# The last two projections of an encoder trunk, as seven block products on pairs of token tiles

## Chip, core, metric

The kernel runs on one core of a Trainium2 chip. The metric is the device time of one execution in microseconds, the median of the runs. The core's engines are TensorE (PE in the profile: matmuls; PEld: its weight loads), VectorE (DVE), ScalarE (ACT), GpSimd (POOL) and SyncE (SP), which here only issues transfers. Each engine works through its own instructions in order.

## What is computed

The reference is a two-layer encoder trunk on 2048 + 256 tokens of 1024 channels, in f32. Cut to the part that is touched, the end of layer 1 (mixer C, its output projection, the residual, and the gate of the per-layer embedding):

```
y = (mixed * c_scale) * silu(g)                  # mixer C
h = h + y @ w_out                                # output projection, 1024 x 1024
gate = sigmoid(rms_norm(h, norm_ple[1]) @ w_ple_gate[1])       # the last gate, 1024 x 1024
out = h + gate * (p[1] @ w_ple_proj[1])          # the last product is made early, and kept in DRAM
```

Layer 0 ends with the same gate on its own weights, and its result is the `h` that mixer C reads.

## The kernel before

Tokens are worked on in 18 tiles of 128 (`P`). Every f32 matrix product is made of three matmuls: each operand is held as a rounded high part and the remainder, a low part, and `mm3` (L177 to L179) adds high times high, high times low and low times high in PSUM. A split is a cast on ScalarE and a subtraction on VectorE (`split_ps` for results in PSUM, L117 and L118; `split_w` for weights, L127 and L128, with a gain L130 and L131) or both on GpSimd (`split_po`, L121 and L122).

Three stages stand at the end of the program, and the order of their work is that in which a scheduler has put the code's instructions on each engine:

- The first gate's loop (layer 0, from about 2366 to 2610 us): a token tile takes 48 matmuls of 512 columns (`gate_half`, L945 on, twice 24 into `po` and `pf`) and eight transposes of the next tile's normed rows. `norm_rows` is a Square with a sum on ScalarE (L184), and on GpSimd a small scale (L109), a power (L112) and the scaling of the tile (L186).
- Mixer C (to about 3035 us): nine blocks of 256 tokens, four channel groups each. Its result goes to DRAM as high and low halves (`ycT_d`).
- The final stage, `out_ple` (L1021 to L1066): for each token tile, `head` makes the output projection in 48 matmuls (two halves of the columns into `pa`), VectorE adds it to the residual `xr` (L1048), the sum is normed and transposed, and `gate_half` makes 48 matmuls of the gate (L957 the sigmoid, L958 and L959 the product with `pp` and the sum). The loop works on the projection of the next tile and the gate of this one by turns.

So the final stage has 18 x 96 = 1728 matmuls of 128x512. The matmul's tiles stand in the trace as `pa<-wh,yh`: PSUM tile, then the streamed weights and the stationary activations. In this stage the weights lie in pools opened on the left side of the memory; `yh` and `yl` come from `work`, a pool on the right; `nh` and `nl` come from the pool `opw1`, on the left. In the first gate's loop weights and activations both lie on the right.

## Time and profile before

| what | value |
|---|---|
| three runs | 3454.49, 3457.00, 3457.43 us, median 3457.0 us |
| the profiled execution | 3456.42 us, of which the span of instructions is 3454.6 us |
| TensorE | busy 3389.5 us, 98% of the span, mean granted clock 0.996 |
| VectorE, ScalarE, GpSimd | busy 57%, 49%, 49% |

The times of single instructions below all come from the one profiled execution, so a sum of them is to be held against its 3456.42 us: the span plus 1.8 us around it. Shares of busy time are averages over very different stages, and what bounds a stage is read in that stage.

### The profile page before, as it was taken

Reading aid. Unit: us, or ns where it says so; the run is one execution under the profiler, and the core shown is the slowest. Engines: PE = TensorE matmul, PEld = TensorE weight load, DVE = VectorE, ACT = ScalarE, POOL = GpSimd, SP = SyncE. Lnnn points to the kernel's source line nnn. Section 1 sums busy time; section 2 is a strip of 40 time slices with the busy share of each in tenths; the row PEclk is TensorE's granted clock in tenths of the full one; section 3 lists DMA queues with packets and bytes.
Section 4 is the critical chain, followed back from the end, with each engine's and each line's share of the span. In section 5 each row is a group of like instructions: output and inputs, shape, how many; then the busy total and the mean of one; then the engine's idle time right before and its main releaser. Section 6 shows DMA issues by size and latency. Waiting matters only on the chain.

```text
span 3454.6 us, 60128 instructions
## 1 busy us (share of the span) xinstructions
PE 3389.5 (98%) x21694; PEld 3020.9 (87%) x21694; DVE 1974.1 (57%) x4298; ACT 1675.6 (49%) x3100; POOL 1694.9 (49%) x1997
## 2 busy tenths in 40 slices
PE   9999999999999999999999999998999999999999
PEld 8998999998899988888888887886889999988887
DVE  5346666667767677768779788773434222342222
ACT  4325666666666666546767776552324111221111
POOL 6774545454645455446777777761113445420000
PEclk9999999999999999999999999999999999999999
DMA  9654323234423324664445635337534122353332
GB/s 289 200 165 137 109 79 105 85 104 126 143 81 100 90 77 123 173 190 124 134 133 158 177 97 140 126 95 258 177 130 158 61 74 68 103 166 111 116 110 73
DMA packets 473969, 446.12 MB, mean 129 GB/s; under 512 B 34504, under 2 KB 414920, under 8 KB 472648
## 3 DMA queue, kind: packets, MB, share of 16 engines
q1 hardware_dynamic: 473672, 442.28, 41.7%
q8 instruction: 172, 2.82, 0.3%
q14 instruction: 125, 1.02, 0.1%
HBM read 277.53 MB, written 164.63 MB: 128 GB/s over the span
## 4 chain that ended last, share of the span: by engine, by line
PE 88%; DVE 4%; DMA 3%; issue 2%; ACT 1%; POOL 1%; SPq 0%; DVEq 0%; ACTq 0%; POOLq 0%
PE pf L177 10%; PE pf L178 10%; PE pf L179 10%; PE pt L369 9%; PE pa L407 6%; PE pa L408 6%; PE po L177 6%; PE po L178 6%; PE po L179 6%; PE pa L177 4%; PE pa L178 4%; PE pa L179 4%; PE po L501 3%; PE po L500 3%; DVE s L653 1%
## 5 line engine op out<-in xcount | busy, mean ns | idle before, releaser
L419 ACT ACTIVATE s<-s,mx 128x1024 f32<-128x1024 f32 x512 | 585.7, 1147 | 172.9 <-DVE mx L653 88.0
L377 DVE TENSOR_TENSOR pl<-pt,ph 128x512 fp32r<-128x512 f32 x780 | 524.1, 686 | 202.3 <-ACT ph L373 194.1
L373 ACT CAST ph<-pt 128x512 fp32r<-128x512 f32 x780 | 437.0, 584 | 261.6 <-PE pt L369 126.5
L369 PE MATMUL pt<-ident,s 128*128 128x128 f32 x3120 | 467.3, 273 | 5.7 <-DVE pl L377 4.5
L369 PEld LDWEIGHTS pt<-ident,s 128*128 128x128 f32 x3120 | 369.5, 140 | 56.6 <-issue 7.0
L653 DVE CUSTOM_DVE_ANT_0 s<-pa,dist,mx 128x512 f32<-128x512 f32 x384 | 286.2, 746 | 51.1 <-PE pa L408 36.1
L673 POOL TENSOR_TENSOR s<-s 128x1024 f32<-128x1024 f32 (+1 forms) x136 | 315.2, 2335 | 0.2
L109 POOL TENSOR_SCALAR rstd<-ss 128x1 f32<-128x1 f32 (+1 forms) x64 | 15.5, 242 | 605.4 <-ACT xn L184 583.6
L482 POOL TENSOR_SCALAR s<-s,rs 128x1024 f32<-128x1024 f32 (+1 forms) x272 | 298.0, 1107 | 12.1
L472 DVE TENSOR_SCALAR_CACHE_REDUCE s<-pa,mx 128x512 f32<-128x512 f32 x384 | 286.1, 745 | 23.1 <-PE pa L408 13.9
L500 PE MATMUL po<-ph,vA 128*128 128x256 f32 x1040 | 282.2, 293 | 0.6 <-ACT ph L373 0.6
L501 PE MATMUL po<-pl,vA 128*128 128x256 f32 x1040 | 279.5, 295 | 1.1 <-DVE pl L377 1.1
L177 PE MATMUL pf<-xh,wh 128*128 128x256 f32 x944 | 265.5, 281 | 2.5 <-DMA xh<-xTh_d 2.5
L178 PE MATMUL pf<-xl,wh 128*128 128x256 f32 x944 | 266.2, 282 | 0.2 <-DMA xl<-xTl_d 0.2
L179 PE MATMUL pf<-xh,wl 128*128 128x256 f32 x944 | 265.3, 281 | 0.0
L407 PE MATMUL pa<-kk,q 128*128 128x512 f32 (+1 forms) x528 | 220.1, 419 | 14.5 <-DMA q<-qTl_d 6.0
L407 PE MATMUL pa<-kA,q 128*128 128x512 f32 (+1 forms) x528 | 222.3, 421 | 3.5 <-DVE s L472 3.3
L112 POOL TENSOR_TENSOR rstd<-rstd,mhalf 128x1 f32<-128x1 f32 (+3 forms) x154 | 164.6, 1069 | 110.5 <-DVE rstd L111 93.3
L958 DVE TENSOR_TENSOR sg<-pp,sg 128x512 f32<-128x512 f32 x72 | 49.8, 692 | 289.8 <-ACT sg L957 284.9
L408 PE MATMUL pa<-kA,q 128*128 128x512 f32 (+1 forms) x528 | 208.1, 394 | 0.0
L408 PE MATMUL pa<-kk,q 128*128 128x512 f32 (+1 forms) x528 | 207.3, 395 | 0.1
L500 PEld LDWEIGHTS po<-ph,vA 128*128 128x128 f32 x1040 | 196.9, 189 | 10.4 <-ACT ph L373 1.0
(240 smaller groups left out, 9753.2 us busy)
## 6 DMA issues: line engine op xcount, KB each, us to landing
xr<-h_d SPq DMA_DIRECT2D x54, 512.0 KB, 3.3
q<-qTh_d SPq DMA_DIRECT2D x144, 128.0 KB, 3.0
q<-qTl_d SPq DMA_DIRECT2D x144, 128.0 KB, 3.0
xh<-xTh_d SPq DMA_DIRECT2D x18, 1024.0 KB, 5.4
xl<-xTl_d SPq DMA_DIRECT2D x18, 1024.0 KB, 8.2
h_d<-xr SPq DMA_DIRECT2D x72, 256.0 KB, 3.6
pp_d<-xr SPq DMA_DIRECT2D x72, 256.0 KB, 2.3
pp<-pp_d SPq DMA_DIRECT2D x36, 512.0 KB, 3.8
```

Source lines behind the costliest of these rows:

```text
L177: pe.matmul(out, lhsT=lhs[0], rhs=rhs[0], start=first, stop=False)
L178: pe.matmul(out, lhsT=lhs[0], rhs=rhs[1], start=False, stop=False)
L179: pe.matmul(out, lhsT=lhs[1], rhs=rhs[0], start=False, stop=last)
L369: pe.transpose(pt[:, (c * 2 + i) * P : (c * 2 + i + 1) * P], s[:, (c0 + c) * P : (c0 + c + 1) * P], ident)
L373: ac.copy(ph, pt)
L377: ve.tensor_tensor(out=pl, in0=pt, in1=ph.bitcast(F32), op=ALU.subtract)
L407: pe.matmul(ps, lhsT=q1, rhs=k[:, i * 512 : i * 512 + w], start=True, stop=False)
L408: pe.matmul(ps, lhsT=q2, rhs=k[:, i * 512 : i * 512 + w], start=False, stop=True)
L419: ac.activation(s[:, c], s[:, c], AF.Exp, bias=bias, scale=-1.0, accum_out=sums[i])
L500: pe.matmul(ov[0][:, 0:256], lhsT=v, rhs=ph[:, c], start=c0 + c == 0, stop=False)
L501: pe.matmul(ov[0][:, 0:256], lhsT=v, rhs=pl[:, c], start=False, stop=c0 + c == nk - 1)
L653: ve.tensor_tensor_reduce(out=s[:, c : c + w], in0=ps, in1=dist[:, off + c : off + c + w], op0=ALU.add, op1=ALU.min, scale=slope, scalar=3 ...
```

## The change

The fused final stage is replaced by two passes over nine pairs of token tiles: first the output projection of all pairs (`n` = 0), whose sum `h` is written back to `h_d`, then the gate of all pairs (`n` = 1), which loads it again. In each pass a pair's 256x1024 times 1024x1024 product is cut into 2x2 blocks, where the two rows of blocks are the pair's two tiles, and made by Strassen's scheme (Winograd's form) with seven products of 128 tokens, 512 channels and 512 columns instead of eight. A product is 4 chunks of 3 matmuls, so a pair takes 84 matmuls of 128x512, and both passes 18 x 84 = 1512.

For that, sums and differences of blocks are needed on both sides. Those of the weights (`t0` to `t3`, four for each matrix) are made on GpSimd in `halves_sums`, called in eight steps of the first gate's loop, written to DRAM, and loaded and split like weights by `block_w`. The 28 split chunks of the gate's blocks go into the tiles of the output projection's, each as soon as its last use, in the last pair of the first pass, is over. The sums of the activations (`s1` to `s4`) are made in `Pair.prepare`: in the first pass on GpSimd, with the low parts on VectorE, in the second on VectorE from the transposed rows in PSUM, with the low parts on GpSimd. `Pair.use` adds the products up, mostly on VectorE, and `Pair.end` makes sigmoid (ScalarE), product with `pp` (GpSimd) and the last sum (VectorE). Mixer C stores its result as one f32 tensor (no `split_po`), and `xn` has two buffers.

The diff, cut to its core:

```diff
-    ycT_d = [dscratch(f"ycT{i}_d", [D, T]) for i in "hl"]
+    ycT_d = dscratch("ycT_d", [D, T])
+    t_d = [[dscratch(f"t{n}{i}_d", [512, 512]) for i in range(4)] for n in "og"]
...
+    def part(src, low):
+        hi, lo = (work.tile([P, 512], F32R, tag=f"a{x}", name=f"a{x}", bufs=8) for x in "hl")
+        ac.copy(hi, src)
+        low.tensor_tensor(out=lo, in0=src, in1=hi.bitcast(F32), op=ALU.subtract)
+        return hi.rearrange("p (c t) -> p c t", t=P), lo.rearrange("p (c t) -> p c t", t=P)
...
+        return [part(quarter(xn, k), ve) for k in range(2)]
...
+    w_tail = ins["w_out_c"][0], ins["w_ple_gate"][1]
+    def halves_sums(pool, n, c):
+        q = []
+        for i in range(4):
+            k, a = divmod(i, 2)
+            b = pool.tile([P, 512], F32, tag=f"q{i}", name="q", bufs=2)
+            sy.dma_start(b, w_tail[n][k * 512 + c * P : k * 512 + c * P + P, a * 512 : a * 512 + 512])
+            if n:
+                ac.activation(b, b, AF.Copy, scale=gple[1][:, k * 4 + c : k * 4 + c + 1])
+            q.append(b)
+        b11, b12, b21, b22 = q
+        for i, (out, x, y) in enumerate(((b11, b12, b11), (b12, b22, b12), (b22, b22, b11), (b21, b21, b22))):
+            po.tensor_tensor(out=out, in0=x, in1=y, op=ALU.subtract)
+            sy.dma_start(t_d[n][(0, 2, 1, 3)[i]][c * P : c * P + P], out)
...
+    BLK = ["11", "21", "t1", "t0", "22", "t3", "t2"]
+    HOME = dict(zip(BLK, ((0, 0), (1, 0), (1, 4), (2, 0), (2, 4), (3, 0), (3, 4))))
...
+    def block_w(n, b):
+        got = []
+        for c in range(4):
+            hi, lo = pair_w(HOME[b][0], HOME[b][1] + c)
+            st = slot()
+            if b[0] == "t":
+                sy.dma_start(st, t_d[n][int(b[1])][c * P : c * P + P])
+                ac.copy(hi, st)
+                (po if c % 2 else ve).tensor_tensor(out=lo, in0=st, in1=hi.bitcast(F32), op=ALU.subtract)
+            else:
+                k, a = int(b[0]) - 1, int(b[1]) - 1
+                sy.dma_start(st, w_tail[n][k * 512 + c * P : k * 512 + c * P + P, a * 512 : a * 512 + 512])
+                split_w(st, hi, lo, gple[1][:, k * 4 + c : k * 4 + c + 1] if n else None)
+            got.append((hi, lo))
+        return got
...
+        def prepare(self):
+            t0, n = self.t0, self.n
+            self.xr, xn = [], []
+            for tq in (t0, t0 + P):
+                self.xr.append(loaded(tq))
+                if not n:
+                    y = work.tile([P, D], F32, tag="xn", name="yc")
+                    sy.dma_start(y.rearrange("p (c t) -> p c t", t=P), chans(ycT_d, tq, P))
+                    xn.append(y)
+            if n:
+                xn = [norm_rows(work, x) for x in self.xr]
+            yield
+            def at(i, k):
+                return quarter(xn[i], k) if n else xn[i][:, k * 512 : k * 512 + 512]
+            e, low = (ve, po) if n else (po, ve)
+            a21 = at(1, 0)
+            if n:
+                t = temp()
+                ac.copy(t, a21)
+                a21 = t
+            yield
+            a11 = at(0, 0)
+            self.a11 = part(a11, ve)
+            s3 = temp()
+            e.tensor_tensor(out=s3, in0=a11, in1=a21, op=ALU.subtract)
+            yield
+            a22 = at(1, 1)
+            s2 = temp()
+            e.tensor_tensor(out=s2, in0=a22, in1=s3, op=ALU.subtract)
+            e.tensor_tensor(out=a21, in0=a22, in1=a21, op=ALU.add)
+            self.s2 = part(s2, low)
+            self.s1 = part(a21, low)
+            self.a22 = part(a22, ve)
+            yield
+            a12 = at(0, 1)
+            self.a12 = part(a12, ve)
+            e.tensor_tensor(out=s2, in0=a12, in1=s2, op=ALU.subtract)
+            self.s3 = part(s3, low)
+            yield
+            self.s4 = part(s2, low)
+            yield
...
+        def end(self, g, i, a):
+            cols, x, t = slice(a * 512, a * 512 + 512), self.xr[i], self.t0 + i * P
+            ac.activation(g, g, AF.Sigmoid)
+            (ve if self.last and a == 0 else po).tensor_tensor(out=g, in0=self.pp[i][:, cols], in1=g, op=ALU.mult)
+            def late():
+                ve.tensor_tensor(out=x[:, cols], in0=x[:, cols], in1=g, op=ALU.add)
+                sy.dma_start(rows(yout, t, P)[:, cols], x[:, cols])
+            after.append(late)
...
+            if m == 1:
+                self.u = gsum()
+                ac.copy(self.u, ps)
+                if not n:
+                    plus(x[0][0], x[0][0])
+            elif m == 2:
+                if n:
+                    g = gsum()
+                    plus(g, self.u)
+                    self.end(g, 0, 0)
                 else:
-                    WG += load_w(wp[g], ins["w_ple_gate"][layer][k : k + 512], 512, [(0, D)], "wg",
-                                 gple[layer][:, k // P : k // P + 4])
-
-            def head(tq):
-                yh = work.tile([P, KC, P], F32R, tag="yh", name="yh")
-                yl = work.tile([P, KC, P], F32R, tag="yl", name="yl")
-                load2(yT, (yh[:, :kc], yl[:, :kc]), lambda d: d[k0:D, tq : tq + P].rearrange("(c p) t -> p c t", p=P))
-                xr = work.tile([P, D], F32, tag="xr", name="xr", bufs=NXR)
-                sy.dma_start(xr, h_d[tq : tq + P])
-                for a in (0, 512):
-                    ps = pa()
-                    for c in range(kc):
-                        mm3(ps, (yh[:, c], yl[:, c]), (WO[c][0][:, a : a + 512], WO[c][1][:, a : a + 512]), c == 0, c == kc - 1)
-                    ve.tensor_tensor(out=xr[:, a : a + 512], in0=ps, in1=xr[:, a : a + 512], op=ALU.add)
-                    if a == 0:
-                        yield
-                yield xr, norm_rows(work, xr, 1)
-
-            nxt = list(head(0))[1]
-            for tq in range(0, T, P):
-                xr, xn = nxt
-                nh = pw.tile([P, KC, P], F32R, tag="nh", name="nh", bufs=1)
-                nl = pw.tile([P, KC, P], F32R, tag="nl", name="nl", bufs=1)
-                step = head(tq + P) if tq + P < T else iter((None, None))
-                next(step)
-                transpose_rows(xn, nh, nl, 0)
-                nxt = next(step)
-                sg = [pw.tile([P, D], F32, tag="sg", name="sg", bufs=1)]
-                for a, pg in ((0, po_()), (512, pf_())):
-                    gate_half(pw, layer, WG, (nh, nl), tq, a, pg, sg, xr, dst(tq))
-
-
-    with pool_ as ws:
-        wp += [ws.enter_context(tc.tile_pool(name=f"wc{g}", bufs=1, reuse_waits="tile")) for g in range(1, 4)]
-        pc = ws.enter_context(tc.tile_pool(name="plc", bufs=1, reuse_waits="tile"))
+                    plus(x[0][0], x[0][0])
+            elif m == 6:
+                plus(self.u, self.u)
+                if not n:
+                    plus(x[1][0], x[1][0], self.u, po)
+            elif m == 5:
+                self.v = gsum()
+                plus(self.v, self.u)
+                if not n:
+                    plus(x[0][1], x[0][1], self.v, po)
+                    plus(x[1][1], x[1][1], self.v, po)
+            elif m == 3:
+                if n:
+                    g = gsum()
+                    plus(g, self.v)
+                    self.end(g, 0, 1)
+                else:
+                    plus(x[0][1], x[0][1])
+                    sy.dma_start(h_d[self.t0 : self.t0 + P], self.xr[0])
+            elif m == 4:
+                to = self.u if n else x[1][0]
+                plus(to, to)
+                if self.last:
+                    self.end(to, 1, 0)
+            elif n:
+                plus(self.u, self.u)
+                if not self.last:
+                    self.end(self.u, 1, 0)
+                plus(self.v, self.v)
+                self.end(self.v, 1, 1)
+            else:
+                plus(x[1][0], x[1][0])
+                plus(x[1][1], x[1][1])
+                sy.dma_start(h_d[self.t0 + P : self.t0 + 2 * P], self.xr[1])
...
+    pairs = [Pair(n, t0) for n in range(2) for t0 in range(0, T, 2 * P)]
...
+    ahead_c = (lambda: None, lambda: begin(BLK[:1], 0), lambda: begin(BLK[1:3], 4), lambda: begin(BLK[3:5], 2))
...
-                split_po(mx[:, :, :cnt], yh[:, :, :cnt], yl[:, :, :cnt])
-                store2(ycT_d, (yh[:, :, :cnt], yl[:, :, :cnt]),
-                       lambda d: d[g * 256 : g * 256 + 256, t0 - 8 + oa : t0 - 8 + ob].rearrange("(m p) t -> p m t", p=P))
+                sy.dma_start(ycT_d[g * 256 : g * 256 + 256, t0 - 8 + oa : t0 - 8 + ob].rearrange("(m p) t -> p m t", p=P), mx[:, :, :cnt])
...
+    begin(BLK[5:], 0)
+    for i, p in enumerate(pairs):
+        step = pairs[i + 1].prepare() if i + 1 < len(pairs) else iter(())
+        order = list(zip((1, 2, 6, 5, 3, 4, 7), BLK))
+        for m, b in order[:5] + order[:4:-1] if p.last else order:
+            a = getattr(p, {1: "a11", 2: "a12", 6: "s2", 5: "s1", 3: "s4", 4: "a22", 7: "s3"}[m])
+            ps = {2: po_, 4: po_, 5: pf_, 7: pf_}.get(m, pa)()
+            for c in range(4):
+                mm3(ps, (a[0][:, c], a[1][:, c]), W[p.n][b][c], c == 0, c == 3)
+            flush_()
+            if m == 1 and p.n:
+                p.embedding()
+            p.use(m, ps)
+            if m != 2:
+                next(step, None)
+            if p.n == 0 and pairs[i + 1].n:
+                W[1][b] = block_w(1, b)
+    flush_()
```

On TensorE, the final stage of before: the end of a gate half, the projection's first half with the transposes behind it, and the start of the gate (`yh`, `yl`, `nh`, `nl` as above).

```order
L179 MATMUL pf<-wh,nl 128x512
L177 MATMUL pa<-wh,yh 128x512 [waits DMAHW0_49]
L178 MATMUL pa<-wl,yh 128x512
L179 MATMUL pa<-wh,yl 128x512 [waits DMAHW1_49]
...
L199 MATMUL pt<-ident,xn 128x128 [waits Pool_49]
L199 MATMUL pt<-ident,xn 128x128 x3
L199 MATMUL pt<-ident,xn 128x128 [waits PE_49]
L199 MATMUL pt<-ident,xn 128x128 x3
L177 MATMUL pa<-wh,yh 128x512
...
L177 MATMUL po<-wh,nh 128x512 [waits Activation_49]
L178 MATMUL po<-wl,nh 128x512
L179 MATMUL po<-wh,nl 128x512 [waits DVE_49]
```

The same engine in the change, a pair of the second pass, from the end of its fifth product (`pa`) over the sixth (`po`) and the seventh (`pf`) to the first of the next pair (`ah` and `al` are the parts of a block or a sum of blocks of activations).

```order
L180 MATMUL pa<-wh,al 128x512
L984 MATMUL pt<-ident,xn 128x128 [waits PE_49]
L984 MATMUL pt<-ident,xn 128x128 x3
L178 MATMUL po<-wh,ah 128x512 [waits DVE_49]
L179 MATMUL po<-wl,ah 128x512
L180 MATMUL po<-wh,al 128x512
...
L984 MATMUL pt<-ident,xn 128x128 [waits Activation_49]
L984 MATMUL pt<-ident,xn 128x128 x3
L178 MATMUL pf<-wh,ah 128x512 [waits DVE_49]
...
L178 MATMUL pa<-wh,ah 128x512 [waits Activation_49]
L179 MATMUL pa<-wl,ah 128x512
L180 MATMUL pa<-wh,al 128x512 [waits DVE_49]
```

The next pair's transposes stand in three groups near the end of a pair (the first group, of eight, is a few rows above this piece), no longer in one per tile, and all matmuls take their activations from `work`.

On GpSimd, two steps of the first gate's loop before: nothing but the norm (in the final stage its rows are the same).

```order
L109 TENSOR_SCALAR rstd<-ss 128x1 [waits Activation_49]
L112 TENSOR_TENSOR rstd<-rstd,mhalf 128x1 [waits Pool_49]
L186 TENSOR_SCALAR xn<-xr,rstd 128x1024 [waits DMAHW0_49,PE_49,Pool_49]
L109 TENSOR_SCALAR rstd<-ss 128x1 [waits Activation_49]
L112 TENSOR_TENSOR rstd<-rstd,mhalf 128x1 [waits Pool_49]
L186 TENSOR_SCALAR xn<-xr,rstd 128x1024 [waits DMAHW1_49,PE_49,Pool_49]
```

The same loop in the change, where the block sums of the weights (`q`) begin.

```order
L187 TENSOR_SCALAR xn<-xr,rstd 128x1024 [waits DMAHW1_49,PE_49,Pool_49]
L1041 TENSOR_TENSOR q<-q 128x512 [waits DMAHW4_49,DMAHW5_49,DMAHW3_49,DMAHW6_49,DMAHW2_49,DMAHW7_49,DMAHW1_49,DVE_49]
L1041 TENSOR_TENSOR q<-q 128x512 [waits DMAHW4_49,DMAHW7_49,DVE_49,Pool_49]
L1041 TENSOR_TENSOR q<-q 128x512 [waits DMAHW0_49,PE_49,Pool_49]
...
L1041 TENSOR_TENSOR q<-q 128x512 [waits DMAHW4_49,DMAHW1_49,DMAHW0_49]
L1041 TENSOR_TENSOR q<-q 128x512 [waits DMAHW6_49,DMAHW4_49,Pool_49]
L1041 TENSOR_TENSOR q<-q 128x512 [waits Pool_49]
L110 TENSOR_SCALAR rstd<-ss 128x1 [waits Activation_49]
L113 TENSOR_TENSOR rstd<-rstd,mhalf 128x1 [waits Pool_49]
L187 TENSOR_SCALAR xn<-xr,rstd 128x1024 [waits DMAHW6_49,PE_49,Pool_49]
```

Eleven of the 32 subtractions now stand in one piece between two norms; five of those between the dots are left out.

On GpSimd again, the change where the second pass begins (`wl<-st,wh` is the low part of a chunk of weights, `al<-tmp,ah` that of a sum of activations, `xr<-g,xr` a sum of the first pass).

```order
L1183 TENSOR_TENSOR xr<-g,xr 128x512
L1100 TENSOR_TENSOR wl<-st,wh 128x512 [waits DMAHW1_49,PE_49,Activation_49]
L1100 TENSOR_TENSOR wl<-st,wh 128x512 [waits DMAHW3_49,PE_49,Activation_49]
L110 TENSOR_SCALAR rstd<-ss 128x1 [waits Activation_49]
L977 TENSOR_TENSOR al<-tmp,ah 128x512 [waits Activation_49]
L113 TENSOR_TENSOR rstd<-rstd,mhalf 128x1 [waits Pool_49]
L977 TENSOR_TENSOR al<-tmp,ah 128x512 [waits Activation_49]
L1100 TENSOR_TENSOR wl<-st,wh 128x512 [waits DMAHW5_49,PE_49,Activation_49]
L187 TENSOR_SCALAR xn<-xr,rstd 128x1024 [waits PE_49,Pool_49]
L977 TENSOR_TENSOR al<-tmp,ah 128x512 [waits Activation_49]
L977 TENSOR_TENSOR al<-tmp,ah 128x512 [waits PE_49,Activation_49]
```

Low parts of weights, of activations and the norm's three steps now share this queue, where before the norm alone stood.

## Rows read from the trace of the kernel before

**Rows 1.** The page: busy times, then the chain that ended last.
```profile
PE 3389.5 (98%) x21694; PEld 3020.9 (87%) x21694; DVE 1974.1 (57%) x4298; ACT 1675.6 (49%) x3100; POOL 1694.9 (49%) x1997
...
PE 88%; DVE 4%; DMA 3%; issue 2%; ACT 1%; POOL 1%; SPq 0%; DVEq 0%; ACTq 0%; POOLq 0%
```

**Rows 2.** Windows: start:end, length; busy us of PE, PEld, DVE, ACT, POOL; clock.
```profile
2366.50:2645.00 278.50, 268.11 (x1358) 226.33 (x1357) 119.12 (x204) 100.88 (x200) 49.44 (x75) 0.99 0.53 176
2645.00:3035.00 390.00, 390.00 (x3348) 390.00 (x3348) 110.85 (x240) 80.53 (x142) 188.80 (x242) 1.00 0.25 81
3035.00:3454.60 419.60, 414.30 (x1877) 339.53 (x1875) 108.23 (x163) 68.96 (x119) 43.79 (x62) 1.00 0.37 112
```

**Rows 3.** TensorE's waits from 3035 us on: us in total, times, longest.
```profile
PE po L177 <- ACT nh L117: 0.3, 1, 0.3
```

**Rows 4.** Timeline of TensorE: start us, length us, instruction; rows of one tile.
```profile
3199.16 0.39 PE L177 MATMUL po<-wh,nh 128*128 128x512 f32 x1
...
3201.88 0.39 PE L177 MATMUL pf<-wh,nh 128*128 128x512 f32 x1
...
3207.32 0.39 PE L177 MATMUL pa<-wh,yh 128*128 128x512 f32 x1
...
3212.92 1.03 PE L199 MATMUL pt<-ident,xn 128*128 128x128 f32 x8
...
3214.03 0.39 PE L178 MATMUL pa<-wl,yh 128*128 128x512 f32 x1
...
3230.30 0.39 PE L177 MATMUL pa<-wh,yh 128*128 128x512 f32 x1
```

**Rows 5.** Timeline of TensorE: first and last matmul of the final stage.
```profile
3035.32 0.40 PE L177 MATMUL pa<-wh,yh 128*128 128x512 f32 x1
...
3449.20 0.39 PE L179 MATMUL pf<-wh,nl 128*128 128x512 f32 x1
```

**Rows 6.** Groups by line from 3035 us on: busy us, mean ns of one.
```profile
L1048 DVE TENSOR_TENSOR xr<-pa,xr 128x512 f32<-128x512 f32 x36 | 24.9, 691 | 122.2 <-PE pa L179 122.2
L186 POOL TENSOR_SCALAR xn<-xr,rstd 128x1024 f32<-128x1024 f32 x18 | 20.3, 1127 | 1.9
L117 ACT CAST nh<-pt 128x512 fp32r<-128x512 f32 x36 | 19.3, 590 | 90.1 <-PE pt L199 90.1
L184 ACT ACTIVATE xn<-xr 128x1024 f32<-128x1024 f32 x18 | 19.1, 1061 | 95.8 <-issue 79.5 <-DVE xr L1048 16.4
L112 POOL TENSOR_TENSOR rstd<-rstd,mhalf 128x1 f32<-128x1 f32 x18 | 9.9, 549 | 1.5
```

**Rows 7.** Splits by source line: ns at least, median, at most; first and last.
```profile
L122 POOL TENSOR_TENSOR yl<-mixd,yh x36: 1239/1290/1764, 2640.4 to 3050.3; 128x512 fp32r<-128x512 f32 x28, 128x496 fp32r<-128x496 f32 x4, 128x528 fp32r<-128x528 f32 x4
L127 ACT CAST wh<-st x16: 610/622/626, 3002.5 to 3021.5; 128x512 fp32r<-128x512 f32 x16
L128 DVE TENSOR_TENSOR wl<-st,wh x16: 670/690/1527, 3003.1 to 3022.8; 128x512 fp32r<-128x512 f32 x16
L130 ACT ACTIVATE wh<-st,gple x32: 709/723/732, 2323.3 to 3047.1; 128x512 fp32r<-128x512 f32 x32
L131 DVE SCALAR_TENSOR_TENSOR wl<-st,gple,wh x32: 737/751/1571, 2324.7 to 3049.0; 128x512 fp32r<-128x512 f32 x32
```

**Rows 8.** Timelines of VectorE, then GpSimd, over the same stretch.
```profile
3037.62 5.25 DVE L131 SCALAR_TENSOR_TENSOR wl<-st,gple,wh 128x512 fp32r<-128x512 f32 x4 [1.78 <-ACT wh L130]
...
3039.44 4.59 POOL L1132 TENSOR_TENSOR zz<-zz 128x536 f32<-128x536 f32 x3
```

**Rows 9.** TensorE's waits in the first gate's loop, 2360 to 2640 us.
```profile
PE po L177 <- ACT sg L957: 4.2, 1, 4.2
PE pt L199 <- POOL xn L186: 1.8, 2, 1.0
```

**Rows 10.** Timelines of ScalarE and VectorE: the last instructions.
```profile
3449.63 0.60 ACT L957 ACTIVATE sg<-pf 128x512 f32<-128x512 f32 x1 [1.67 <-PE pf L179]
...
3450.26 0.69 DVE L958 TENSOR_TENSOR sg<-pp,sg 128x512 f32<-128x512 f32 x1 [0.78 <-ACT sg L957]
```

More of the change, by code (lines that the diff above doesn't have):

```diff
@@ L1011, in trunk_kernel @@
         else:
-            x0 = [work.tile([P, KC, NB], F32R, tag=t, name="x0") for t in ("yh", "yl")]
-            transpose_rows(xn, *x0, 0)
-            xn = norm_rows(work, loaded(P), 1)
+            first_x.append(norm_rows(work, loaded(P)))
         gate_half(pw, 0, WG0, n_, tq, 512, pf_(), sg, xr[0], h_d[tq : tq + P])
@@ new lines, in trunk_kernel, with begin @@
+    pairs = [Pair(n, t0) for n in range(2) for t0 in range(0, T, 2 * P)]
+    W = [{}, {}]
+    first_step = pairs[0].prepare()
+    def begin(blocks, steps):
+        for b in blocks:
+            W[0][b] = block_w(0, b)
+        for _ in range(steps):
+            next(first_step)
+    ahead_c = (lambda: None, lambda: begin(BLK[:1], 0), lambda: begin(BLK[1:3], 4), lambda: begin(BLK[3:5], 2))
+    for g in range(1, 4):
+        load_c(g)
+    with tc.tile_pool(name="plc", bufs=1, reuse_waits="tile") as pc:
@@ L1070, in trunk_kernel @@
         edge = pc.tile([P, 4, 16], F32, name="edge")
         sy.dma_start(edge, ins["pool_edge"].rearrange("w e -> (w e)").partition_broadcast(P).rearrange("p (w e) -> p w e", e=16))
-        for g in range(1, 4):
-            load_c(wp[g], g)
         zc = pc.tile([P, 4, 2, 16], F32, name="zc")
@@ L1077, in chain @@
         def chain(t0):
-            xh = work.tile([P, KC, NB], F32R, tag="yh", name="xh")
-            xl = work.tile([P, KC, NB], F32R, tag="yl", name="xl")
-            for tt in range(NB // P):
-                transpose_rows(norm_rows(work, loaded(t0 + tt * P), 1), xh, xl, tt * P)
-            return xh, xl
+            return turned2([norm_rows(work, loaded(t0 + tt * P)) for tt in range(2)])
         ZW = NB + 24
```

114 lines of the change are left out of this document (77 added, 37 removed).

## Prediction, made before the changed kernel was run

> **What bounds the kernel now.** I read the page first: TensorE is busy 98% of the span, and the chain that ended last runs 88% through it [rows 1]. That is an average, so I went to windows by stage. In the final stage TensorE works 414.30 of 419.60 us at full clock, while VectorE, ScalarE and GpSimd work 108.23, 68.96 and 43.79 [rows 2], and the waits name one single stall, of 0.3 us [rows 3]. So this stage ends when its matmuls end, and nothing else is near a limit: an operation less on TensorE is time saved, one more elsewhere is free until it makes a matmul wait. Mixer C before it is as full (390.00 of 390.00); the first gate's loop has some holes (268.11 of 278.50).
>
> The timeline gives the stage's prices [rows 4]. A gate's matmul takes (3201.88 - 3199.16) / 12 = 0.2267 us from start to start, a projection's (3212.92 - 3207.32) / 24 = 0.2333. The eight transposes take 3214.03 - 3212.92, less one matmul, = 0.88 us. One tile is then 48 x 0.2333 + 48 x 0.2267 + 0.88 = 22.96 us, and the trace has 3230.30 - 3207.32 = 22.98. Eighteen tiles make 413.3; from the first to the end of the last matmul [rows 5] are 3449.20 + 0.23 - 3035.32 = 414.1.
>
> **The change, term by term.**
>
> *Matmuls.* 216 of 1728 go, and 1512 are left. Which price do they have? The two prices differ with where the tiles lie: `yh` comes from the pool on the right and the weights from the left, `nh` lies on the same side as the weights. All activations of the new products come from the right and all weights from the left, as in the projection. So I take 0.2333 for all: 352.7 us, with the bound 0.2267: 342.8. The transposes are as many as before, 18 x 0.88 = 15.8. The passes take 368.6 instead of 413.3: **44.7 less** (54.7 at the lower price). The naive saving, 216 matmuls at the mean, would be 49.7; 5 of it are lost because the gate's matmuls fall to the dearer price.
>
> *Work of the other engines in a steady pair.* Nearest rows: a VectorE operation 0.69 (L1048), a cast 0.59, a Square 1.06, a GpSimd scaling 1.13 and power 0.55 [rows 6], a sigmoid 0.60 [rows 10], a GpSimd operation on two tensors 1.29 (L122) [rows 7]. A pair of the first pass lasts 84 x 0.2333 = 19.6 us on TensorE, and has 15 VectorE operations (10.4 us), 8 on ScalarE (4.7), 7 on GpSimd (9.0). One of the second lasts 21.4 and has 18 on VectorE (12.4), 9 casts and copies, two Squares and four sigmoids on ScalarE (9.8), and on GpSimd 8 operations and two norms (10.3 + 3.4 = 13.7). All are hidden as sums. As a chain: after a pair's last product come a sum, a sigmoid, two GpSimd products and then, behind them in the queue, the norm of a tile of the next pair: 0.69 + 0.60 + 2.58 + 1.68 = 5.6 us into the next pair, and that tile's transposes stand some 13 us in. Cover 7 us; I cost it at 1 us in all for small holes (bounds 0 and 5).
>
> *The turn from the first pass to the second.* Here 28 chunks of weights are split into tiles in use until then. On ScalarE 12 x 0.72 + 16 x 0.62 = 18.6 us, on VectorE 12 x 0.75 + 8 x 0.69 = 14.5, on GpSimd 8 x 1.29 = 10.3 [rows 7]. Time for it is from the end of the last first-pass pair's first product to the start of the next pair's seventh: 12 products and 16 transposes, 12 x 12 x 0.2333 + 1.8 = 35.4 us. In it the engines also have about 6/7 of a pair of each pass: VectorE 19.5, ScalarE 12.4, GpSimd 19.5. The sums are 34.0, 31.0 and 29.8 of 35.4: nearly full on three engines at once, and a block that comes late stops TensorE.
>
> And the prices are those of an operation alone. Four splits of VectorE took 5.25 us, 1.31 each, while GpSimd added tensors next to them; alone one takes 0.75. GpSimd's sums took 4.59 / 3 = 1.53 there [rows 8]. Both engines read both operands from SBUF. Operations with an operand in PSUM, most of the pairs' work, keep their 0.69. In the turn 20 splits of VectorE are of the kind that was slowed, beside a GpSimd that is busy nearly all the time: 20 x 0.56 = 11.2 more, 45.2 of 35.4. **I take 9 us lost, once.** Bounds: 0 without the slowing (34.0 fits), and 24 if each split waits out one whole GpSimd operation (34.0 + 20 x 1.29 = 59.8).
>
> The Trainium skill, page "SBUF — State Buffer", section "SBUF: two separate sides", says that VectorE with two SBUF inputs and a GpSimd operation reading SBUF exclude each other: whoever starts first holds the shared ports for its whole instruction, and the other is fully blocked. The slowed rows agree; by the rule the turn would lie nearer the upper bound than mine.
>
> *The block sums in the first gate's loop.* GpSimd gets 32 subtractions of 1.29, 41 us over eight steps of 48 x 0.2267 + 0.88 = 11.8. Spread evenly that is 5.2 + 1.7 of 11.8, hidden. But eleven stand in one piece, 14.2 us, longer than a step, with the next norm queued behind, and behind the norm the transposes of the next tile. Two buffers of `xn` give one step of cover. This loop already loses 4.2 and 1.8 us to such waits [rows 9]. I take **4 us**; bounds 0 and 12, a whole step. The 64 transfers for it on SP, whose stores wait for GpSimd with the loads of the loop behind them, could lose that same step, and are in these bounds.
>
> *Mixer C.* GpSimd loses its splits and SP a store per group; TensorE was full there, so nothing is gained. Its end still hides 20 of the 28 splits of the first pass (before, the projection's 16 stood there too [rows 7]); the last 8 come after it, needed 14 us later. I take **1 us** (0 to 5).
>
> *The end.* Before, the last matmul is followed by sigmoid 0.60, product 0.69, sum and store [rows 10]. Now a sum (0.69) stands ahead of the sigmoid, and the column half before it has its product on GpSimd (1.29) and its sum in the same VectorE queue: about 0.69 + 0.69 + 0.6 = **2 us** (0.7 to 3.3).
>
> Sum: -44.7 + 1 + 9 + 4 + 1 + 2 = **-27.7**. Against the profiled execution 3456.4 - 27.7 = 3428.7; the median stands 0.6 above that execution, so 3429.
>
> **The rivals.**
>
> - *All is hidden* (as the bare sums have it): -44.7 + 2 and little more, about 3415. For it: every sum fits. Against it: three engines at 84 to 96% in the turn, and the slowed splits. Chance 0.18.
> - *The products keep the cheaper price* of 0.2267: 10 less than the forecast, 3419. Against it: the side on which the tiles lie is as in the dearer rows. Chance 0.06.
> - *The ports exclude each other in the turn*: each of the 20 splits meets a whole GpSimd operation, 24 instead of 9: 3444. For it: the most that a split took is 1.53 (L128) and 1.57 (L131), about twice its median [rows 7]. Against it: that is +0.8, not +1.29, and GpSimd isn't always just starting. The Trainium skill's page named above would have it so. Chance 0.15.
> - *GpSimd sets the pace of the second pass* (slower): its queue runs in order, products that wait for sigmoids hold up the norm and the low parts of the next pair. It decides from the point where its 13.7 us per pair, with waits, exceed 21.4 by 3.1 (9 x 3.1 = 28, the whole gain), so at 24.5. If each of its 12 large operations is slowed by 0.47, the most that L122 stands above its median [rows 7], it has 19.3, which fits; it needs 0.9 each, or 5 us of idle waiting as well. At 25.3 the time is 3429 + 9 x 3.9 = 3464. Chance 0.09.
>
> **Numbers.** The forecast has the remaining 0.52, with its own range 3420 to 3440. For 8 in 10 I reach from the hidden case, 3412, to just above the excluded ports, 3447, and leave out the slower case and the tails. What a measurement of this kernel can tell from no change is about 0.2%, 7 us. All cases but the last are faster by more than that, less some 0.03 where high bounds meet: faster 0.88, within 0.04, slower 0.08.
>
> **What would show it.** TensorE's matmuls 216 fewer; from the first product to the last some 370 us plus waits; starts 0.233 apart inside a product. In the waits, a cluster at the fifth to seventh products of the second pass's first pair, released by low parts of weights; VectorE's splits there above 1 us. In the first gate's loop one or two waits on `xn` after the eleven subtractions. Second-pass pairs 21.4 apart: if they are 23 or more, GpSimd's queue or the ports set the pace, and the forecast is wrong; if the first-pass pairs are longer than 19.6, the price of the matmuls is.

## The result, and the profile after

The changed kernel takes 3418.64 us (median of 4 runs, 3417.92 to 3424.23), the kernel before on the same chip 3455.74 (4 runs, 3451.59 to 3457.43). The ratio is 0.9898, with a 95% interval of 0.9881 to 0.9915: 37 us faster. The forecast was 3429, 28 us faster, with a range of 3412 to 3447. Direction and range hold; 9 us of the gain were not foreseen, and the rows say where they lie.

The page of the profiled execution (3424.23 us, span 3422.4) has the same head as before [rows 1]: busy times, then the chain that ended last.

```profile
PE 3348.8 (98%) x21478; PEld 2981.5 (87%) x21478; DVE 2123.2 (62%) x4461; ACT 1766.1 (52%) x3257; POOL 1882.1 (55%) x2106
...
PE 84%; DMA 5%; DVE 4%; issue 2%; POOL 2%; ACT 2%; SPq 0%; DVEq 0%; ACTq 0%; POOLq 0%
```

TensorE has 216 matmuls less and is still the bound; the other three engines have gained 91 to 187 us of work, and 4% of the chain has passed from TensorE to transfers and the others. The windows of the change by stage show where it is full: start:end, length, busy time of PE, PEld, DVE, ACT, POOL (in brackets the instructions), then clock, DMA share, GB/s. They are the first gate's loop, mixer C, the first pass without its end, and the rest of the two passes.

```profile
2371.20:2610.10 238.90, 235.89 (x1108) 195.49 (x1108) 104.20 (x138) 79.72 (x146) 79.75 (x87) 1.00 0.67 230
2610.10:3035.50 425.40, 421.69 (x3594) 420.74 (x3593) 137.57 (x307) 111.70 (x214) 151.17 (x198) 1.00 0.24 77
3035.50:3201.20 165.70, 165.70 (x713) 133.54 (x712) 104.96 (x143) 50.48 (x86) 97.58 (x70) 1.00 0.55 179
3201.20:3414.40 213.20, 205.69 (x943) 165.05 (x941) 134.61 (x179) 95.06 (x170) 138.24 (x128) 0.99 0.47 149
```

The first pass has no hole at all (165.70 of 165.70). The turn and the second pass lose 7.5 of 213.20 us, and the clock stays at its upper level throughout (0.99 to 1.00).

Single executions of one kernel differ by some us in the part ahead of the first gate's loop, which the change hardly touches: 2361.2 to 2373.2 us in the thirteen profiles of the table (e2, another version of before, is told at its place). So stages are compared, each from its own first matmul to that of the next; the passes to the end of their last matmul; the tail from there to the end of the span. In us, worked out from the timelines of TensorE:

```
                        up to loop   loop   mixer C   passes   tail
before                    2369.1    243.5    422.8    414.1     5.1
the change                2371.2    238.9    425.4    378.9     8.0
difference                  +2.1     -4.6     +2.6    -35.2    +2.9   = -32.2
forecast                            +4        +1      -34.7    +2     = -27.7
the change, e5            2361.2    238.4    425.0    378.9     8.0
the change, e9            2363.6    238.6    426.3    377.8     8.0
e1  pad of 32 bytes       2368.5    238.5    433.2    373.9     8.0
e3  stored from g         2371.8    239.4    426.6    372.3     8.0
e10 the same again        2373.2    238.3    422.3    372.3     8.0
e4  no turn               2368.4    238.7    426.3    370.6     8.3
e6  both cures            2369.2    241.5    427.7    387.0     9.3
e7  no block sums         2369.2    238.3    423.0    378.4     8.0
e8  one normed tile       2369.2    238.5    426.5    376.9     8.0
e11 an eighth product     2366.3    239.0    424.8    419.9     6.0
e12 products on VectorE   2362.8    238.7    425.1    371.4     7.5
```

The profiled pair differs by 32.2 us and the medians by 37; the first column alone, which swings by 12 us, can make that difference.

The stages' borders are not quite those of the work. In the change four matmuls of the passes already run inside mixer C (at 3001 us), which leaves 1508 of the 1512 to the passes and gives mixer C 0.9 us; and four transposes that stand in the loop before (1112 instructions there, 1108 in the change) stand in mixer C, some 0.4 us.

**The passes.** The timeline of TensorE in the change, in a pair of the first pass: start, length, instruction. The two rows are 12 matmuls apart; the third is the last matmul of the program.

```profile
3096.19 0.40 PE L178 MATMUL po<-wh,ah 128*128 128x512 f32 x1
...
3098.99 0.40 PE L178 MATMUL pa<-wh,ah 128*128 128x512 f32 x1
...
3414.16 0.40 PE L180 MATMUL po<-wh,al 128*128 128x512 f32 x1
```

(3098.99 - 3096.19) / 12 = 0.2333 us from start to start, the projection's price of before [rows 4]. TensorE's waits from 3035.5 us on are these: us in all, times, longest.

```profile
PE pt L984 <- POOL xn L187: 5.3, 6, 2.7
PE pt L984 <- ACT tmp L1145: 1.0, 1, 1.0
PE pf L179 <- POOL wl L1100: 0.8, 1, 0.8
PE pf L178 <- ACT wh L1099: 0.3, 1, 0.3
```

Where one stall of 0.3 us stood [rows 3] there are nine, of 7.4 us together. Only two of them, 1.1 us, wait for a weight. Most wait for a normed tile `xn`, ahead of the transposes.

From pair to pair the first products of the second pass are 25.3, 22.1, 22.2, 22.2, 25.8, 21.3, 21.3 and 21.9 us apart (21.3 is a pair without a wait, transposes included), where the pairs of the first pass take 19.6.

### The profile page after: what moved, and what is told of

Its sections match the earlier page's. It is cut to its first block, busy times and chain, and to the rows that moved or that the text cites. A ratio compares the mean times of both kernels' runs of the same rounds, so it can differ in the third digit from the quotient of the medians.

```text
span 3422.4 us, 60525 instructions
## 1 busy us (share of the span) xinstructions
PE 3348.8 (98%) x21478; PEld 2981.5 (87%) x21478; DVE 2123.2 (62%) x4461; ACT 1766.1 (52%) x3257; POOL 1882.1 (55%) x2106
## 4 chain that ended last, share of the span: by engine, by line
PE 84%; DMA 5%; DVE 4%; issue 2%; POOL 2%; ACT 2%; SPq 0%; DVEq 0%; ACTq 0%; POOLq 0%
PE pf L178 10%; PE pf L180 10%; PE pf L179 10%; PE pt L370 9%; PE pa L408 6%; PE pa L409 6%; PE po L178 5%; PE po L180 5%; PE po L179 5%; PE po L502 3%; PE po L501 3%; PE pa L178 3%; PE pa L179 3%; PE pa L180 3%; DMA xr<-h_d 1%
## 5 line engine op out<-in xcount | busy, mean ns | idle before, releaser
L501 PEld LDWEIGHTS po<-ph,vA 128*128 128x128 f32 x1040 | 197.5, 190 | 10.3 <-ACT ph L374 1.0
L502 PEld LDWEIGHTS po<-pl,vA 128*128 128x128 f32 x1040 | 197.8, 190 | 7.0 <-DVE pl L378 3.0
L178 PE MATMUL pf<-wh,xh 128*128 128x512 f32 (+1 forms) x576 | 195.4, 339 | 0.3 <-DVE vl L596 0.3
L180 PE MATMUL pf<-wh,xl 128*128 128x512 f32 (+1 forms) x576 | 194.6, 338 | 0.0
L179 PE MATMUL pf<-wl,xh 128*128 128x512 f32 (+1 forms) x576 | 194.4, 337 | 0.0
L479 POOL TENSOR_TENSOR sm<-sm 128x1 f32<-128x1 f32 x128 | 26.2, 204 | 290.1 <-ACT s L420 289.8
```

Source lines behind the costliest of these rows:

```text
L178: pe.matmul(out, lhsT=lhs[0], rhs=rhs[0], start=first, stop=False)
L179: pe.matmul(out, lhsT=lhs[0], rhs=rhs[1], start=False, stop=False)
L180: pe.matmul(out, lhsT=lhs[1], rhs=rhs[0], start=False, stop=last)
L501: pe.matmul(ov[0][:, 0:256], lhsT=v, rhs=ph[:, c], start=c0 + c == 0, stop=False)
L502: pe.matmul(ov[0][:, 0:256], lhsT=v, rhs=pl[:, c], start=False, stop=c0 + c == nk - 1)
```

## The experiments

Twelve runs, each held against the kernel before on the same chip. Edits are against the changed kernel unless another is named.

**Runs of the change alone (e5, e9).** No edit: they give the change's own spread, e5 on the chip of e6 to e8, e9 on that of e10 to e12 (e1 to e4 share a chip without one).

> The change once more, as the kernel that the others of this group are held against, since differences of 4 us are in question: 3418 to 3420 by its earlier runs.

> The change, as the kernel that the next three are held against on the same chip: 3418 to 3421.

Measured: 3420.69, ratio 0.9907 (0.9894 to 0.9921), and 3422.27, 0.9904 (0.9889 to 0.9919). With the first run the change lies at 0.990 to 0.991 three times, and its passes at 377.8 to 378.9.

**e1: where the operands lie.** The prediction gave all matmuls 0.2333 because activations lie on the right of the memory and weights on the left. A pad of 32 bytes moves the right side's tiles without changing sides.

```diff
+    pad = ctx.enter_context(tc.tile_pool(name="pad", bufs=1, side="right", reuse_waits="tile"))
+    ve.memset(pad.tile([P, 8], F32, tag="pad", name="pad", bufs=1), 0.0)
```

> The change with 32 bytes per partition reserved ahead of the pool that holds the activations on the right side, so that all of them (and the first gate's weights, which lie on the same side) move by 32 bytes; nothing else differs. Theory one: the dearer price of a matmul (0.2333 against 0.2267 us) hangs on how its two operands lie to each other, and the shift puts them alike: 1512 x 0.0066 = 10 us less, and starts 0.2267 apart in both passes; in mixer C, whose matmuls of 256 columns start 0.1167 apart, perhaps something too. Rival: the price hangs on the side, the PSUM tile or which operand is streamed: no difference.

Measured: 3423.94, ratio 0.9906 (0.9893 to 0.9920). Two stretches of its TensorE timeline: 12 matmuls of a pass, and 48 of mixer C, 256 wide.

```profile
3011.41 0.28 PE L178 MATMUL pf<-ah,wh 128*128 128x256 f32 x1
...
3017.17 0.28 PE L178 MATMUL po<-ah,wh 128*128 128x256 f32 x1
...
3099.54 0.39 PE L178 MATMUL po<-wh,ah 128*128 128x512 f32 x1
...
3102.26 0.39 PE L178 MATMUL pa<-wh,ah 128*128 128x512 f32 x1
```

The 48 of mixer C in the change itself:

```profile
3013.12 0.28 PE L178 MATMUL po<-ah,wh 128*128 128x256 f32 x1
...
3018.72 0.28 PE L178 MATMUL pf<-ah,wh 128*128 128x256 f32 x1
```

In the passes the price falls from 0.2333 to 2.72 / 12 = 0.2267, with both sides as they were: the side is not the reason, the addresses are. The first gate's loop, whose two operands both lie on the right and move together, keeps its 2.72 us for 12 matmuls and its length (238.5); so it seems to be how the two lie to each other. In mixer C the same shift makes the price rise, from 5.60 / 48 = 0.1167 to 5.76 / 48 = 0.1200, and that stage is some 7 us longer (433.2). The passes win only 4 to 5 of the 10 us that 1512 matmuls should give, since the waits on `xn` grow from 5.3 to 8.4 us. In all nothing is gained.

**e3, e10: when a tile's buffer comes free.** In the change the last sum is written into `xr` and stored from there, so the tile is held until its store has landed.

```diff
-                ve.tensor_tensor(out=x[:, cols], in0=x[:, cols], in1=g, op=ALU.add)
-                sy.dma_start(rows(yout, t, P)[:, cols], x[:, cols])
+                ve.tensor_tensor(out=g, in0=x[:, cols], in1=g, op=ALU.add)
+                sy.dma_start(rows(yout, t, P)[:, cols], g)
```

> The change with the last sum of the second pass written into the gate's tile and stored from there, so that the buffer of the residual is free when it has been read, not when the store has landed. Theory one: the waits of the second pass on normed rows (4.8 us in the profile) come from the ring store, buffer free, load of the next tile, norm: about 5 us less, second-pass pairs 21.4 us apart. Rival (the one of the prediction): GpSimd's queue sets it: no difference, and the waits stay.

> The last sum stored from the gate's tile, once more beside the change, since 4 to 6 us are at the edge of what two separate groups tell apart. If the ring of store, free buffer and load is what makes the second pass wait: 4 to 6 us less than the change beside it. If the first result was chance: no difference.

Measured: 3414.89, ratio 0.9880 (0.9866 to 0.9893), and 3416.03, the same ratio and interval; the second is 6.2 below e9 on the same chip. The passes take 372.3 both times, 5.5 to 6.6 less than the change. TensorE's waits of e10 from 3195 us on:

```profile
PE pf L178 <- DVE g L1183: 1.0, 1, 1.0
PE pt L984 <- POOL xn L187: 0.6, 2, 0.3
PE pf L179 <- POOL wl L1100: 0.6, 1, 0.6
PE po L179 <- POOL wl L1100: 0.6, 1, 0.6
PE pt L984 <- ACT tmp L1145: 0.5, 1, 0.5
```

The waits on `xn` fall from 5.3 to 0.6 us. The first pair of the second pass, the turn's own, still takes 25.5, but those behind it 21.9 and then 21.3 each. What this takes away is a wait of the queue of SP, where the load of a tile stands until the store from its buffer has landed. In the change, from 3200 to 3415 us:

```profile
SPq L970 <- DMA out_dram<-xr: 37.6, 13, 3.9
```

In e10 that queue has no such wait. In the change's own timeline (queue of SP, then ScalarE, GpSimd, TensorE) the ring can be followed:

```profile
3264.82 0.34 SPq L1177 DMA_DIRECT2D out_dram<-xr  x1
3267.09 0.32 SPq L970 DMA_DIRECT2D xr<-h_d  x1
3270.36 1.06 ACT L185 ACTIVATE xn<-xr 128x1024 f32<-128x1024 f32 x1 [2.62 <-DMA xr<-h_d]
3272.52 1.39 POOL L187 TENSOR_SCALAR xn<-xr,rstd 128x1024 f32<-128x1024 f32 x1
3273.97 1.09 PE L984 MATMUL pt<-ident,xn 128*128 128x128 f32 x8 [0.70 <-POOL xn L187]
```

The store of a tile is issued at 3264.82; the load into its buffer goes only 2.27 us later; the Square starts 3.27 us after that; the tile's transposes start at 3273.97, 9.15 us after the store. Some 5.5 of the 9.15 us are the two landings; Square, power and scaling make the rest.

**e4: no turn.** The second pass reads the weights of the first, so its 28 chunks are neither loaded nor split, and its products are with the projection's weights instead of the gate's.

```diff
-                W[1][b] = block_w(1, b)
+                W[1][b] = W[0][b]
```

> The change without the turn: the second pass uses the weights of the first, so 28 loads and splits are left out (the result is not the gate's). The prediction's estimate: 9 us less. From the waits in the profile after, added up around the turn, 3 to 4 us less. If VectorE and GpSimd shut each other out of the memory for whole operations: up to 24 less.

Measured: 3414.85, ratio 0.9880 (0.9865 to 0.9895). The passes take 370.6, 7.2 to 8.3 less than the change, and five of the second pass's eight steps, the turn's pair first among them, take 21.3 each. Its only waits:

```profile
PE pt L984 <- POOL xn L187: 2.3, 3, 1.4
```

So the turn costs 7 to 8 us, 4.0 of them in its own pair (25.3 against 21.3; 2.9 and 3.1 in e9 and e5) and the rest in the pairs behind. But the pairs behind wait for `xn` without a turn too: three of the steps take 22.3, 21.8 and 22.9, some 3 us over 21.3. The ring is tight by itself, and the turn makes it worse.

**e7: no block sums.** The 32 subtractions, their loads and stores are left out, and plain blocks of the weights are loaded in the passes.

```diff
-        if tq // P - 6 in range(8):
-            halves_sums(pw, *divmod(tq // P - 6, 4))
...
-                sy.dma_start(st, t_d[n][int(b[1])][c * P : c * P + P])
+                sy.dma_start(st, w_tail[n][int(b[1]) // 2 * 512 + c * P : int(b[1]) // 2 * 512 + c * P + P, int(b[1]) % 2 * 512 : int(b[1]) % 2 * 512 + 512])
```

> The change without the 32 subtractions (and their loads and stores) in the first gate's loop; the second pass and the first load plain blocks in their place, so the sums are not the scheme's. The prediction's estimate: 4 us less. By the profile after, where the loop is 4.6 us shorter than before in spite of them: 0 to 2 less (three transposes in front of a tile's first matmul, some 0.55 us each).

Measured: 3417.78, ratio 0.9897 (0.9884 to 0.9911). The loop takes 238.3, against 238.4 to 238.9 with the sums: they cost at most 0.6 us there.

**e8 and e2: the second buffer of the normed tile.** Both ask whether it is why the loop became shorter. e8 takes it away in the change; e2 gives it to the kernel before.

```diff
-    def norm_rows(pool, xt, nb=2):
+    def norm_rows(pool, xt, nb=2, one=False):
+        if one:
+            pool.tile([P, D], F32, tag="xn", name="xn", bufs=nb)
...
-    n_ = turned(norm_rows(work, xr[0]))
+    n_ = turned(norm_rows(work, xr[0], one=True))
...
-            xn = norm_rows(work, xr[1])
+            xn = norm_rows(work, xr[1], one=True)
```

```diff
...
-            xn = norm_rows(work, xr[1], 1)
+            xn = norm_rows(pw, xr[1], 2)
...
```

> The change with each normed tile of the first gate's loop in the same buffer, so that loop has one, as before. Theory one: the second buffer is what shortened the loop: 4 to 5 us more than the change. Rival: it isn't (parts by half tiles, or the sums' place in the order): no difference.

> The kernel before with two buffers of the normed tile in the first gate's loop (the second in that loop's own pool), nothing else. In the profile the loop takes 238.9 us with the change where it took 243.5, though it got 32 subtractions more. Theory one: the second buffer is what gained it: 4 to 5 us less than before, about 3451. Rival: it comes from the order of the transposes or from single stalls of the two profiled executions: no difference.

Measured: e8 3420.15, ratio 0.9901 (0.9888 to 0.9915), its loop 238.5: the buffer is not the cause. e2 3459.72, 1.0018 (1.0009 to 1.0027). e2 moves the tile into another pool too, and its loop starts at 2400.1 instead of 2369.1 and is 215.6 long, with a new stall of 6.5 us for `xn`; it ends 3 us later than before's. So it says nothing about the buffer alone.

**e11: an eighth product in each pair.** It adds 12 matmuls, whose result is not used, to each of the 18 pairs.

```diff
+            if m == 7:
+                ps8 = pa()
+                for c in range(4):
+                    mm3(ps8, (a[0][:, c], a[1][:, c]), W[p.n][b][c], c == 0, c == 3)
```

> The change with one product of 12 matmuls more in each of the 18 pairs (the seventh made a second time into another PSUM tile that nobody reads), so a pair has as many matmuls as with plain blocks. If TensorE sets the pace of both passes: 18 x 12 x 0.2333 = 50.4 us more, less the 5 or so of waits that the longer pairs cover: 45 to 50 more, slower than the kernel before. If another engine or a transfer sets the pace of a part of the pairs, that part takes the product for nothing: 25 or less.

Measured: 3460.96, ratio 1.0018 (1.0009 to 1.0027), 38.7 above e9, less than the 45 expected: with the 216 matmuls put back, the change is no faster than the kernel before. The passes take 419.9, 42 more than in e9, and the tail 2.0 less, as the extra matmuls run ahead of the last product. First-pass pairs go from 19.6 to 22.4, the full 12 x 0.2333 = 2.8. Nine such are 25.2; the second pass gives only the remaining 17 of 25, since its waits for `xn` were there to be filled:

```profile
PE pt L984 <- POOL xn L187: 2.0, 1, 2.0
```

**e12: GpSimd's products on VectorE.** e10, with four products per pair moved off GpSimd.

```diff
-            (ve if self.last and a == 0 else po).tensor_tensor(out=g, in0=self.pp[i][:, cols], in1=g, op=ALU.mult)
+            ve.tensor_tensor(out=g, in0=self.pp[i][:, cols], in1=g, op=ALU.mult)
```

> As the last sum stored from the gate's tile, and with the gate's four products of a pair on VectorE (0.69 each) in place of GpSimd (1.29). If GpSimd's queue holds up the second pass, as the slower rival of the prediction has it: 3 us or more less than that kernel. If not: no difference, VectorE having 22 operations (15.2 us) of a pair's 21.4.

Measured: 3411.78, ratio 0.9871 (0.9857 to 0.9884), 4.3 below e10 and the fastest of the study. But the passes win 0.9 (371.4) and the tail 0.5; in the profiled executions the largest difference is in the part ahead of the loop (2362.8 against 2373.2), which the edit doesn't touch. What this edit is worth in the medians is therefore not shown; that GpSimd doesn't set the pace of the second pass is.

**e6: both prices and the ring.** It was to give the passes 0.2267 without touching mixer C, by parts of 520 floats of which 512 are used at an offset (32 bytes in the passes), in eight tiles in fixed rotation, with e3's edit and, to make room, the embeddings in halves.

```diff
-        hi, lo = (work.tile([P, 512], F32R, tag=f"a{x}", name=f"a{x}", bufs=8) for x in "hl")
+        k = parts[0] % 8
+        parts[0] += 1
+        hi, lo = (work.tile([P, 520], F32R, tag=f"a{x}{k}", name=f"a{x}", bufs=1)[:, i : i + 512] for x, i in (("h", o), ("l", 8 - o)))
...
```

> The change with its activations laid 32 bytes apart from the other stages' in the two passes alone (so the 512-column matmuls have the 0.2267 of the shift tried before, and mixer C's 256-column ones keep the 0.1167 that the shift took to 0.1200), and with the last sum stored from the gate's tile. The embedding's rows are loaded as halves of the columns to make room. Theory: 1512 x 0.0066 = 10 us from the matmuls and 4 from the waits on normed rows: 3405, if the next chain (GpSimd, VectorE) still fits the pairs of 19.0 and 20.8 us. Rival: a pair is held by other engines as soon as the matmuls are shorter: no more than the 4 us of the second cure, 3415.

Measured: 3437.28, ratio 0.9951 (0.9938 to 0.9963), slower than the change. With tiles 2080 bytes apart the starts lie 0.227 to 0.233 us apart, not at one price, and TensorE waits for operands for which it did not wait before (its longest waits from 3038 us on):

```profile
PE po L178 <- DVE xr L1188: 6.4, 5, 1.7
PE po L178 <- ACT ah L980: 2.7, 2, 1.5
```

Whether the fixed rotation or the halved embeddings bring these waits, no run tells apart. It failed as a cure and settles no rule for the addresses.

## Why the prediction was right or wrong, step by step

*Matmuls, -44.7: right in size, wrong in its reason.* 1512 at 0.2333 and the transposes are 368.6; e4, whose turn is gone, has 370.6, of which some 3 go with its waits on `xn`. The reason given, the side on which tiles lie, fell in e1; the number held because the change happened to leave the addresses as in the dearer rows. The rival of the cheaper price could not come with this layout, and e1 shows that where it comes, mixer C pays it back. e11 confirms the frame of the sum: with nothing but TensorE's work added, the first pass pays to the full, and the gain is gone.

*The turn, 9 once, and the pairs, 1: right in size, in part by luck.* The passes are 378.9 - 368.6 = 10.3 over the bare sum, as forecast (10). The place was right for one half: the turn's own pair loses 4.0 us, and all its waits stand at its fifth to seventh products (0.48, 0.98, 0.29 and 0.85 us, at 3225.2, 3233.0, 3236.1 and 3237.4), though only the last two, 1.1 us, are for weights. The slowing was there, at half the size forecast. VectorE's twenty splits of the turn, from 3185 to 3240 us:

```profile
L132 DVE SCALAR_TENSOR_TENSOR wl<-st,gple,wh 128x512 fp32r<-128x512 f32 x12 | 12.8, 1092 | 2.6 <-ACT wh L131 2.5
L1100 DVE TENSOR_TENSOR wl<-st,wh 128x512 fp32r<-128x512 f32 x8 | 7.4, 922 | 4.3 <-ACT wh L1099 4.3
```

That is 12 x 1.092 + 8 x 0.922 = 20.5 us instead of 14.5: 6.0 more, where 11.2 were forecast. Twelve of the twenty take 0.67 to 0.75, as alone, and eight 1.01 to 1.84. With 6.0 the prediction's own sum is 40.0 of 35.4, 4.6 too much, which is near the 4.0 of the turn's pair. The slowed ones stand beside GpSimd; the rows are of the change's timelines, VectorE (4.04 / 3 = 1.35 and 1.24), then GpSimd (low parts of activations at 1.50).

```profile
3219.51 4.04 DVE L132 SCALAR_TENSOR_TENSOR wl<-st,gple,wh 128x512 fp32r<-128x512 f32 x3
3226.72 1.24 DVE L1100 TENSOR_TENSOR wl<-st,wh 128x512 fp32r<-128x512 f32 x1 [1.96 <-ACT wh L1099]
...
3219.34 3.00 POOL L977 TENSOR_TENSOR al<-tmp,ah 128x512 fp32r<-128x512 f32 x2
```

In front of them ScalarE waits for the transfers of the weights, which the working left out:

```profile
3225.42 1.27 ACT L1099 CAST wh<-st 128x512 fp32r<-128x512 f32 x2 [2.50 <-DMA st<-tg_d]
3235.39 0.62 ACT L1099 CAST wh<-st 128x512 fp32r<-128x512 f32 x1 [1.93 <-DMA st<-tg_d]
```

The other half of the 8 us is not in the turn. A tile that falls behind there meets the ring of buffers, whose store, load and norm take 9 us, so the delay does not die out: the next pairs take 22.1 to 22.2, and one 25.8. e3 and e10 break the ring at one place and get 5.5 to 6.6 us back with all the turn's work left in; some 3 of these the ring costs without a turn too (e4), where the prediction had 1 for the pairs. So the splits were counted too dear and the ring not at all, and the two errors nearly cancel. The chain that I gave 7 us of cover, through sum, sigmoid, products and the norm, was the wrong one: the tight one runs through the landing of a store.

*Rivals for the turn.* Exclusive ports, 24 instead of 9: the stage loses 8, so not. The Trainium skill, page "SBUF — State Buffer", section "SBUF: two separate sides", has the two engines exclude each other; the splits at 1.24 to 1.35 beside GpSimd agree with that, but twelve of the twenty are not slowed, and what the rule did not tell is how little of it would reach TensorE. GpSimd as the pace of the second pass: the mean of the eight steps above is 182.1 / 8 = 22.8, short of the 24.5 at which this would decide, and less work on it (e12) changes the passes by 0.9. By the prediction's own test, pairs of 23 or more, only the turn's pair and one other fail.

*The first gate's loop, +4: the step that failed, with the wrong sign.* It became 4.6 us shorter. The sums are hidden (e7: at most 0.6), so the cost I feared from eleven in one piece is not there. On GpSimd the eleven are no piece of 14.2 us: four run at 2407.32, one at 2413.78, and then

```profile
2415.76 4.23 POOL L1041 TENSOR_TENSOR q<-q 128x512 f32<-128x512 f32 x3 [0.66 <-DMA q<-in_w_out_c_dram]
2429.03 1.29 POOL L1041 TENSOR_TENSOR q<-q 128x512 f32<-128x512 f32 x1 [9.04 <-DMA q<-in_w_out_c_dram]
2430.95 2.65 POOL L1041 TENSOR_TENSOR q<-q 128x512 f32<-128x512 f32 x2 [0.63 <-POOL q L1041]
2434.08 0.19 POOL L110 TENSOR_SCALAR rstd<-ss 128x1 f32<-128x1 f32 x1 [0.47 <-ACT xn L185]
```

The last norm before them ends at 2379.82, so they have 54 us, not a step of 11.8, and wait for their loads in between; the norm behind them starts after an idle GpSimd has waited 0.47 us for ScalarE's Square, not behind the sums. The order of the instructions was read as if it were their time. No wait of the loop in the change is for `xn`. The second buffer of `xn` that I counted as cover is not needed either (e8). What I did not ask is how the order changes on ScalarE at the loop's start. Before, the first sigmoid stands behind weight splits that wait for transfers:

```profile
2406.08 0.91 ACT L130 ACTIVATE wh<-st,gmix 128x256 fp32r<-128x256 f32 x2 [1.39 <-DMA st<-m_d]
2407.69 0.51 ACT L130 ACTIVATE wh<-st,gmix 128x256 fp32r<-128x256 f32 x1 [0.70 <-DMA st<-m_d]
2408.21 1.28 ACT L957 ACT_TABLE_LOAD   x1
2409.51 0.60 ACT L957 ACTIVATE sg<-po 128x512 f32<-128x512 f32 x1
```

In the change it stands ahead of them:

```profile
2405.91 1.54 ACT L976 CAST ah<-pt 128x512 fp32r<-128x512 f32 x3
2407.47 1.28 ACT L958 ACT_TABLE_LOAD   x1
2408.76 0.60 ACT L958 ACTIVATE sg<-po 128x512 f32<-128x512 f32 x1
2409.73 1.70 ACT L131 ACTIVATE wh<-st,gmix 128x256 fp32r<-128x256 f32 x4
```

TensorE's wait for that sigmoid falls from 4.2 us [rows 9] to 1.7. Of the two waits for `xn` in [rows 9] one, of 1.0, lies in the loop, and it is gone; the change's waits in the loop begin so:

```profile
PE po L178 <- ACT sg L958: 1.7, 1, 1.7
PE po L178 <- ACT ah L976: 0.8, 3, 0.3
```

All waits of the loop together fall from 6.0 to 3.2 us, which is 2.8 of the 4.6; 0.4 are the four transposes now in mixer C, and some 1.4 are not traced. That the order gave the 2.5 us at the sigmoid has one experiment on its side. In e7 two of the weight splits stand ahead of the sigmoid again, 0.91 us and a wait of 0.20:

```profile
2404.84 0.91 ACT L131 ACTIVATE wh<-st,gmix 128x256 fp32r<-128x256 f32 x2 [0.20 <-DMA st<-m_d]
```

There TensorE's wait for it is 2.8 us instead of 1.7, longer by these 1.1. But e7 was built for another question and leaves out the sums as well; no run changes the order alone.

*Mixer C, +1: between -0.5 and +3.8* in the runs of the change and those that leave this stage alone (422.3 to 426.6 against 422.8), +2.6 in the profiled one, of which 1.3 is work of the stages beside it. *The end, +2:* 2.9. VectorE's last product, beside one of GpSimd, takes 1.26 instead of 0.69 [rows 10]; and the sum ahead of the last sigmoid starts at 3415.57, 1.2 us after the last matmul, behind two sums of the product before. In e11, where twelve matmuls stand between the two products, the tail is 6.0, 2.0 less. The rows are of VectorE, then GpSimd.

```profile
3416.95 1.26 DVE L1173 TENSOR_TENSOR g<-pp,g 128x512 f32<-128x512 f32 x1 [0.70 <-ACT g L1172]
...
3416.39 1.27 POOL L1173 TENSOR_TENSOR g<-pp,g 128x512 f32<-128x512 f32 x1 [4.61 <-ACT g L1172]
```

So of the 9 us by which the gain is larger than forecast some 8.6 are the loop's; mixer C and the end take 2.5 back, and the rest, some 3 us, lies within the swing of the part ahead of the loop.

## What to carry to other kernels

Price the matmuls that are left by the rows of the same operand layout, not by the mean: here it decided 5 to 10 us, and a shift of 32 bytes moves it. When a one-time burst of work delays a stage, look at the ring that the next tiles must go through (store landed, buffer free, load, norm), for it sets whether the delay is lost once or again in each pair; writing the result elsewhere freed 6 us in two lines. An order of instructions on one engine is not yet a time: eleven in a row waited for their loads and held up nothing. And where an edit moves instructions in front of a stage, read the order on every engine at the start of that stage: the sign of the loop's term seems to have lain there, not in the work added.

## What the runs showed of the hardware

A matmul's interval depends on how its operands' addresses lie: 32 bytes of shift make the 512-wide ones 0.2267 instead of 0.2333 and the 256-wide ones 0.1200 instead of 0.1167 (e1). Where both operands move by the 32 bytes, in the first gate's loop, the interval stays 0.2267 (e1). With tiles 2080 bytes apart both prices appear within one pass (e6). Which bits decide, and why the two widths go opposite ways, stays open.
